# A streaming encoder layer: residual loads, decay rows, head 0 and one head unit change places

## The chip, the core and the metric

The kernel runs on one core of a Trainium2 chip. A core has a matrix engine (TensorE, PE in the profile), a vector engine (DVE), an activation engine (ACT), a general engine (POOL) and a sync engine (SP). Each takes its instructions in the order of its own queue. DMA is issued from the queues of SP, ACT and POOL and carried by 16 DMA engines. The metric is device microseconds of one execution; the time of a kernel is the median of its runs.

## What is computed

One layer of a hybrid encoder with one set of weights, for two request groups: a prompt of 1024 positions and a running stream ("sample") of 32 positions with a cache of 256. Both are handled as 1056 columns of feature-major data.

```
h   = x * (1 + sc1) + sh1
mq, mk, mv, mo, mi, mf, fq, fk, fv, ff, gu, gv = split(h @ w_in)
hm  = mlstm(mq, mk, mv, ...)                    # 4 heads of 64, chunks in sequence
hf  = softmax(fq @ fk.T / 8 + F[t] - F[s]) @ fv # 8 heads of 64, F = cumsum of log forget values
hg  = gu * spatial_gate(layer_norm(gv))
mix = concat(hm, hf, hg) @ w_o
x   = layer_norm(ALPHA * x + (1 + g1) * mix)
y   = (silu(h2 @ w_gate) * (h2 @ w_up)) @ w_down   # h2 = x * (1 + sc2) + sh2
x   = layer_norm(ALPHA * x + (1 + g2) * y)
```

For the sample, the keys, values and log forget values of the cache stand ahead of the new ones, so F there is a running sum over 256 + 32 positions for each of 8 heads. The forgetting attention is called fox in the kernel.

## The kernel before

Nearly every product is made in float32 accuracy from two rounded parts: an operand is split into a high part (a cast, on ACT) and a low part (a subtraction, on DVE), and `gemm` (L110 to L118) makes three matmuls of each 128-row slice. Weights come through `weights` (L92): a load on SP into one of three raw buffers, the cast (L104), the subtraction (L105).

The 1056 columns are two groups: group 0 is positions 0 to 511, group 1 is positions 512 to 1023 and the 32 sample columns. The work goes in phases.

**First phase** (the loop over `ORDER` in `run`). Tokens of `ORDER` are steps: `q3` computes queries and keys of fox head 3 for group 0 (`head_unit`), `f3` is that head's attention over group 0, `g` is the next part of the gates (log forget values, stabilisers), `k0`, `v`, `o`, `G1` and so on are units of the input projection, `s` prepares the mLSTM states, `m0` to `m3` are mLSTM chunks, `a` is a part of the modulation vectors. Results wait in DRAM: `dqh` and `dql` hold queries and keys of the heads, `dv` the values, `dM` the stabiliser rows of the mLSTM, `dmix[c]` the mixers' output of group c, in 8 slices of 128 rows (k = 0, 1 are mLSTM, 2 to 5 fox, 6 and 7 the spatial gate). `head_unit` also makes group 1's part for heads 0 and 1 (`QD = 2`).

**Output projection of group 0** (in `run`, after `s2.close()`). `wo_mix(0, ...)` (L991) loads slices of `dmix[0]` and splits them, six of them first (2, 3, 4, 6, 7, 5), then slices 0 and 1, which come last from the mixers. `wo_res` loads the residual `z` from `xT`, two loads of 1 MB. Between them stand the group 1 units of the fox heads `QD` to `PRE - 1`, that is heads 2 and 3: `fm_unit` (L235) makes a head's queries and keys over 544 columns in 48 matmuls of 272 columns, and `evac_qk` (L358) splits them, stores them in `dqh` and `dql`, and stores the keys as an output. With `act=False` the sum of the two parts and the output store are on POOL, with `act=True` (heads from `PRE` on) on ACT. `wo_range` (L1038) makes the projection in 8 blocks of 128 rows over 256 columns, three PSUM banks deep; `sublayer_end` (L1052) adds the residual, takes a pivot off and sums for the layer norm. The second 256 columns are interleaved with the norm of the first (`ln1`, L1070: scale, shift, modulation, and a new split into operands at L1086 and L1087). The norm of the second half follows, and then the group 1 units of heads `PRE` to 7, which have nothing to do with it.

**Mixers of group 1** (`mixers`) beside the MLP of group 0. After `s1.close()` the memory of the first phase is reused for the attention of group 1. `fox_sample` is the sample's attention: it makes the running sums of the cache's log forget values with a triangular matmul (L853), writes the rows F and -F to DRAM (`dsf`), and reads them back as extra rows of keys and queries (`kn`, `q`, `kc`). Then `fox(h, ...)` runs for heads 0 to 7, for five of them with an mLSTM chunk woven in. The tiles q2, qp, k2 and v have one buffer each there (`foxbufs = (2, 1, 1, 1, 2)`), k1 has two; the sample's q, kn and vc use the tags q2, qp and v. Units of the MLP (`up`, `down`) stand behind the mixers in the program and are PE's filler.

Engines' queues are put in order when the program is built: instructions are taken by priority (program order, with 200 places of advance for steps f and m) as they come ready in a simulated timeline. On the chip that order is fixed, and an instruction that waits holds up what stands behind it on its engine. Tiles with the same tag in a pool share that tag's buffers, and a new tile waits until an older one is let go.

Of the kernel before, what the change touches and what calls it, by code (L numbers as in the profile page):

```python
# [7 lines left out]
F32 = mybir.dt.float32  # L8
F32R = mybir.dt.float32r
AF = mybir.ActivationFunctionType  # L10
ALU = mybir.AluOpType
# [4 lines left out]
P = 128  # L16
D = 1024
KT = 8
S = 1024
T = 1056  # L20
NS = 32
PAST = 256

GO = (0, 512)
GN = (512, 544)
# [6 lines left out]
UPF = 0  # L32
LWE = 1
NB = (3, 2, 2)
PRE = 4
T1 = (1, 1, 0, 2)
XB, AB = (3, 6)
HPA = 200
MLB = (1, 2, 3, 4, 5)
RESE = "pp"  # L40
TAFF = ("aaaaaaaa", "aaaaaaav")
ORDER = "q0 f0 g q1 a f1 a g q2 f2 k0 k1p s a q3 f3 a v q4 f4 a q5 f5 o a m0 G0 q6 f6 a m1 G1p G2p q7 m2 f7 a m3 G3"
FP = (0, 0)
RAW = 3
WB = 3
# [9 lines left out]
def weave(*parts):  # L55

    parts = list(parts)
    while parts:
        for p in list(parts):
            if next(p, parts) is parts:  # L60
                parts.remove(p)
# [6 lines left out]
class Kernel:  # L68
# [10 lines left out]
    def t(self, pool, shape, dt=F32, tag=None, bufs=None):  # L79
        self.n += 1  # L80
        kw = {} if bufs is None else {"bufs": bufs}
        return pool.tile(shape, dt, tag=tag, name=f"{self.phase}_{tag}_{self.n}", **kw)
# [755 lines left out]
        self.store(self.dmix[c][64 * (h % 2):64 * (h % 2) + 64, 2 + h // 2, o:o + nq], r[:, :nq])  # L838


    def fox_sample(self):
        self.phase = "foxs"
        nc, d = self.nc, self.d
        t = lambda shape, tag, bufs=1, dt=F32: self.t(self.mx, shape, dt, tag, bufs)
        N = PAST + NS
        lf = t([P, 2, 8], "lfc")
        self.load(lf, d["cache_lf"])
        lp = t([P, 2, 96], "q2", self.foxbufs[1])
        nc.gpsimd.memset(lp, 0.0)
        nc.vector.tensor_copy(lp[:, :, 64:72], lf)  # L850
        ps = self.t(self.pt, [P, 512], F32, "t")
        for j in range(2):
            nc.tensor.matmul(ps[:96, j * P:(j + 1) * P], lp[:, j, :], self.tri, start=True, stop=True)  # L853
        fr = t([72, 2, N], "p", 4)
        F = fr[64:72, 0, :]
        nc.vector.tensor_copy(F[:, 0:P], ps[64:72, 0:P])
        nc.vector.tensor_scalar(F[:, P:PAST], ps[64:72, P:PAST], F[:, P - 1:P], None, ALU.add)
        nc.vector.tensor_scalar(F[:, PAST:], self.sf[64:72, :], F[:, PAST - 1:PAST], None, ALU.add)
        nc.vector.tensor_scalar(fr[64:72, 1, :], F, -1.0, None, ALU.mult)
        self.store(self.dsf, fr[64:72])  # L860
        q = t([66, 8, NS], "q2", self.foxbufs[1])
        kn = t([66, 8, NS], "qp", self.foxbufs[1])
        for x in (q, kn):
            nc.vector.memset(x[64:66], 1.0)
        nc.vector.tensor_copy(kn[0:64], self.qks[64:128])
        nc.vector.tensor_copy(q[0:64], self.qks[0:64])
        self.load(kn[64:65], self.dsf[:, 1, PAST:].unsqueeze(0))
        self.load(q[65:66], self.dsf[:, 0, PAST:].unsqueeze(0))
        vc = t([P, 2, 512], "v", self.foxbufs[3])
        self.load(vc, d["cache_v"])  # L870
        for g in range(2):
            hs = slice(4 * g, 4 * g + 4)
            kc = t([66, 4, PAST], "k1", self.foxbufs[0])
            nc.vector.memset(kc[64:66], 1.0)
            self.load(kc[0:64], d["cache_k"][:, hs, :])
            self.load(kc[64:65], self.dsf[hs, 1, 0:PAST].unsqueeze(0))
            s = self.t(self.pss, [P, 512], F32, "s")
            for x in range(4):
                r = slice(32 * x, 32 * x + 32)
                nc.tensor.matmul(s[r, :PAST], q[:, 4 * g + x, :], kc[:, x, :], start=True, stop=True)  # L880
                nc.tensor.matmul(s[r, PAST:N], q[:, 4 * g + x, :], kn[:, 4 * g + x, :], start=True, stop=True)
            nc.vector.tensor_tensor(s[:, PAST:N], s[:, PAST:N], self.smask, ALU.add)
            m, z = t([P, 2], "fmx", 3), t([P, 2], "fsm", 3)
            m, z = m[:, 0:1], z[:, 0:1]
            nc.vector.tensor_reduce(m, s[:, :N], AX.X, ALU.max, negate=True)
            pr = t([P, N], "p", 4)
            nc.scalar.activation(pr, s[:, :N], AF.Exp, bias=m, accum_out=z)
            nc.vector.reciprocal(z, z)
            nc.vector.tensor_scalar(pr, pr, z, None, ALU.mult)
            ps = self.t(self.pt, [P, 512], F32, "t")  # L890
            for b in range(3):
                w = P if b < 2 else NS
                nc.tensor.transpose(ps[:w, b * P:(b + 1) * P], pr[:, b * P:b * P + w], self.ident)
            pT = t([P, 3, P], "pth", self.foxbufs[4])
            nc.scalar.copy(pT[:, 0:2, :].rearrange("p b q -> p (b q)"), ps[:, 0:256])
            nc.scalar.copy(pT[0:NS, 2, :], ps[0:NS, 256:384])
            o = self.t(self.po, [P, 512], F32, "o")
            for b in range(3):
                w = P if b < 2 else NS
                for x in range(4):  # L900
                    h = slice(256 * g + 64 * x, 256 * g + 64 * x + 64)
                    nc.tensor.matmul(o[32 * x:32 * x + 32, 0:64], pT[:w, b, 32 * x:32 * x + 32],
                                     vc[:, b, h] if b < 2 else self.vs[:, h], start=b == 0, stop=b == 2)
            ob = t([P, 64], "fo")
            nc.scalar.copy(ob, o[:, 0:64])
            nc.tensor.transpose(o[0:64, P:2 * P], ob, self.ident)
            res = t([64, 2, 2, NS], "fo")
            nc.scalar.copy(res.rearrange("p i a q -> p (i a q)"), o[0:64, P:2 * P])
            for a in range(2):
                self.store(self.dmix[1][64 * a:64 * a + 64, 2 + 2 * g:4 + 2 * g, 512:544], res[:, :, a], nc.scalar)  # L910
# [97 lines left out]

    def wo_res(self, c, pool):
        z = self.z[c] = self.t(pool, [P, KT, GN[c]], F32, f"z{c}", 1)  # L1010
        for k in range(0, KT, 4):
            self.load(z[:, k:k + 4], self.d["xT"][k:k + 4, :, GO[c]:GO[c] + GN[c]].rearrange("k p n -> p k n"))

    def wo(self, c, st, cuts, eng, res=None):
        self.phase = f"wo{c}"
# [301 lines left out]
    def mixers(self):  # L1317
        def slow(part):
            for _ in part:
                yield  # L1320
                yield

        self.fox_sample()
        for h in range(8):
            parts = [self.fox(h, ((4, 5), (6, 7)))]
            if h in MLB:
                parts.append(slow(self.mlstm(self.nextm)))
                self.nextm += 1
            weave(*parts)

    def run(self):
        nc, tc, d = self.nc, self.tc, self.d
        dr = self.pool("dr", space=DRAM)
        t = lambda shape, tag: self.t(dr, shape, F32, tag)
# [72 lines left out]
        def emit(x):  # L1407
            eng = nc.gpsimd if x[-1] == "p" else nc.vector
            x = x.rstrip("p")
            i = int(x[1:] or 0)  # L1410
            if x[0] == "g":
                next(gates, None)
                return ()
            if x[0] == "f":
                return self.fox(i, ((0, 1, 2, 3),))
            if x[0] == "m":
                return self.mlstm(i)
            if x[0] == "q":
                self.head_unit(i)
            elif x[0] == "k":  # L1420
                self.fm_unit(w3[i], self.evac_mqk(2 + i, 0.125), eng=eng)
            elif x[0] == "G":
                self.tm_unit(w2[3 + i % 2], 256, (self.evac_gv, self.evac_gmlp)[i % 2],
                             range(4 * (i // 2), 4 + i // 2 * 5), eng=eng)
            elif x[0] == "s":
                self.mlstm_states()
            elif x[0] == "a":
                more(1)
            else:
                self.tm_unit(w2["-vo".index(x)], 256, self.evac_raw((None, self.dmv, self.dmo)["-vo".index(x)]), eng=eng)  # L1430
            return ()

        for x in ORDER.split():
            if x[0] in "fm" and HPA:
# [10 lines left out]
        self.hh, self.hl, self.z = {}, {}, {}  # L1445
        self.operand(0, self.ph)
        self.wo_mix(0, self.KORDER[0][:6])
        self.wo_res(0, self.pz)
        for h in range(QD, PRE):
            self.fm_unit(w3[2 + h], self.evac_qk(h), (1,))  # L1450
        self.wo_mix(0, self.KORDER[0][6:])
        self.pn = self.pool("pn")
        self.ln_consts()
        st = self.ln_begin(nc.vector)
# [6 lines left out]
        weave(self.ln1(0, st, *MM[0][1]))  # L1461
        for h in range(PRE, 8):
            self.fm_unit(w3[2 + h], self.evac_qk(h, True), (1,))
# [83 lines left out]
        n = nj * 256  # L1547
        t = self.t(self.pz, [P, 4, n], F32R, "z0", 1)
        w = self.last_weights(((t[:, 0], t[:, 1]), (t[:, 2], t[:, 3])), (2, 3))
        act2 = dict(act)  # L1550
        for half, (a, b) in enumerate(LN[1][::-1]):
# [6 lines left out]
            else:  # L1558
                h, l = (self.t(pb, [P, KT * 272], F32R, f"{x}{a}", 1) for x in ("ah", "al"))
# [117 lines left out]
```

## Time and profile before

| | us |
|---|---|
| median of three runs | 1371.85 |
| lowest, highest | 1370.64, 1373.48 |
| the profiled execution | 1378.78 |
| its span | 1376.9 |
| PE busy in it | 1337.6 |
| mean granted clock of PE | 0.991 |

The span is the time from the first to the last instruction in the profiled execution. A line of a timeline gives the start and the length in microseconds, the engine, the line of the kernel, the operation with output and input tiles, the shape, and in brackets how long the engine was idle before and who released it. SPq and POOLq are instructions by which an engine issues DMAs. A stretch gives each engine's busy time with the number of instructions, then the granted clock of PE as a share of full clock, the share of the DMA engines that was busy, and what they moved. Tiles carry the name of the phase in which they were made: `tm_ah` and `tm_al` are the two parts of the projection's operand (their memory was made earlier), `wo_z` is the residual.

### The profile page before, as it was taken

The numbers are of one execution on the slowest core, as the hardware profiler recorded it, in microseconds if no ns is written. First come the engines' busy times: TensorE is split into PE (matmuls) and PEld (weight loads), VectorE is DVE, ScalarE is ACT, GpSimd is POOL, SyncE is SP. The second block draws the span as 40 slices with busy tenths as digits, with TensorE's granted clock in tenths as the row PEclk, the third lists the DMA queues.
The fourth block names the chain that finished last, engine by engine and source line by source line (L and its number), as shares of the span: only waits on it lengthen the run. The fifth ranks groups of instructions, "written<-read, shape, count | busy, mean of one in ns | idle before, by whom it ended". The sixth has DMA issues, their size and how long they took to land.

```text
span 1376.9 us, 25164 instructions
## 1 busy us (share of the span) xinstructions
PE 1337.6 (97%) x9434; PEld 1219.9 (89%) x9434; DVE 997.6 (72%) x2129; ACT 658.2 (48%) x1309; POOL 225.2 (16%) x258
## 2 busy tenths in 40 slices
PE   7999999999999989999999999999999999999996
PEld 4898889998899767888888889899999999999995
DVE  5545553679669648777776766778998988889777
ACT  3314454445436544545545455436564454545354
POOL 0202000053133200000000000274610000000341
PEclk9999999999999989999999999999999999999998
DMA  9765565446444774543433423664596658454321
GB/s 359 257 236 151 159 206 155 164 141 201 149 162 142 199 180 151 148 137 117 144 111 101 128 91 97 199 171 125 175 245 180 195 161 222 133 176 129 99 78 66
DMA packets 119210, 221.72 MB, mean 161 GB/s; under 512 B 18508, under 2 KB 62296, under 8 KB 119088
## 3 DMA queue, kind: packets, MB, share of 16 engines
q1 hardware_dynamic: 111760, 207.55, 47.8%
q0 software_dynamic: 5968, 11.80, 5.0%
q8 instruction: 75, 1.23, 0.4%
q10 hardware_dynamic: 1360, 0.76, 0.2%
q14 instruction: 47, 0.39, 0.1%
HBM read 188.13 MB, written 51.85 MB: 174 GB/s over the span
## 4 chain that ended last, share of the span: by engine, by line
PE 84%; DVE 7%; DMA 5%; ACT 2%; issue 1%; SPq 1%; ACTq 0%; DVEq 0%
PE up_g L116 6%; PE up_g L118 6%; PE up_g L117 6%; PE dn_g L116 4%; PE dn_g L118 4%; PE dn_g L117 4%; PE tm_g L281 3%; PE tm_g L282 3%; PE tm_g L283 3%; PE sup_u L118 3%; PE sup_u L116 3%; PE sup_u L117 3%; PE fox_t L815 2%; PE sup_g L117 2%; PE sup_g L118 2%; PE sup_g L116 2%
## 5 line engine op out<-in xcount | busy, mean ns | idle before, releaser
L116 PE MATMUL up_g<-tm_ah,up_whi 128*128 128x512 f32 (+1 forms) x384 | 141.5, 368 | 1.0 <-ACT start_qks L376 1.0
L118 PE MATMUL up_g<-tm_ah,up_wlo 128*128 128x512 f32 (+1 forms) x384 | 142.1, 370 | 0.0
L117 PE MATMUL up_g<-tm_al,up_whi 128*128 128x512 f32 (+1 forms) x384 | 141.6, 369 | 0.0
L1206 ACT CAST sup_whi<-sup_raw 128x1024 fp32r<-128x1024 f32 x54 | 56.0, 1048 | 91.4 <-PE dn_u L117 47.9
L104 ACT CAST up_whi<-up_raw 128x1024 fp32r<-128x1024 f32 x50 | 52.4, 1049 | 77.6 <-PE dn_g L117 30.9
L116 PEld LDWEIGHTS up_g<-tm_ah,up_whi 128*128 128x128 f32 x384 | 73.1, 190 | 12.4 <-ACT start_qks L376 1.2
L118 PEld LDWEIGHTS up_g<-tm_ah,up_wlo 128*128 128x128 f32 x384 | 73.3, 191 | 10.9
L117 PEld LDWEIGHTS up_g<-tm_al,up_whi 128*128 128x128 f32 x384 | 73.1, 190 | 11.1
L105 DVE TENSOR_TENSOR up_wlo<-up_raw,up_whi 128x1024 fp32r<-128x1024 f32 x50 | 66.8, 1336 | 19.5 <-ACT up_whi L104 19.0
L1061 DVE SCALAR_TENSOR_TENSOR wo_z<-dn_g,start_mod,wo_z 128x512 f32<-128x512 f32 (+4 forms) x120 | 60.1, 520 | 25.3 <-PE dn_g L118 24.9
L788 ACT ACTIVATE fox_p<-fox_s,fox_fmx 128x384 f32<-128x384 f32 (+2 forms) x96 | 55.2, 579 | 46.1 <-DVE fox_fmx L786 37.2
L1207 DVE TENSOR_TENSOR sup_wlo<-sup_raw,sup_whi 128x1024 fp32r<-128x1024 f32 x54 | 68.0, 1262 | 10.4 <-ACT sup_whi L1206 10.3
L116 PE MATMUL dn_g<-up_acth,dn_whi 128*128 128x512 f32 (+2 forms) x200 | 73.8, 370 | 0.0
L118 PE MATMUL dn_g<-up_acth,dn_wlo 128*128 128x512 f32 (+2 forms) x200 | 73.2, 366 | 0.0
L117 PE MATMUL dn_g<-up_actl,dn_whi 128*128 128x512 f32 (+2 forms) x200 | 73.2, 367 | 0.0
L104 ACT CAST dn_whi<-dn_raw 128x1024 fp32r<-128x1024 f32 (+1 forms) x44 | 42.7, 970 | 63.2 <-PE up_g L117 19.8
L783 DVE TENSOR_REDUCE fox_fmx<-fox_s 128x1 f32<-128x384 f32 (+2 forms) x96 | 52.6, 553 | 20.7 <-PE fox_s L780 19.3
L820 ACT CAST fox_pth<-fox_t 128x512 fp32r<-128x512 f32 (+1 forms) x80 | 41.3, 544 | 46.9 <-PE fox_t L815 46.6
L821 DVE TENSOR_TENSOR fox_ptl<-fox_t,fox_pth 128x512 fp32r<-128x512 f32 (+1 forms) x80 | 49.4, 631 | 13.0 <-ACT fox_pth L820 12.4
L105 DVE TENSOR_TENSOR dn_wlo<-dn_raw,dn_whi 128x1024 fp32r<-128x1024 f32 (+1 forms) x44 | 49.5, 1124 | 10.9 <-ACT dn_whi L104 10.5
L281 PE MATMUL tm_g<-tm_whi,start_h1h 128*128 128x256 f32 (+1 forms) x192 | 55.6, 290 | 1.7 <-ACT tm_vhl L711 1.7
L281 PE MATMUL tm_g<-tm_whi,start_ah 128*128 128x256 f32 (+1 forms) x192 | 54.3, 286 | 0.7 <-ACT tm_brs L336 0.7
(659 smaller groups left out, 4816.6 us busy)
## 6 DMA issues: line engine op xcount, KB each, us to landing
up_raw<-w_gu SPq DMA_DIRECT2D x50, 512.0 KB
dn_raw<-w_dn SPq DMA_DIRECT2D x28, 512.0 KB
ada_late<-w_ada SPq DMA_DIRECT2D x24, 512.0 KB
sup_raw<-w_gu SPq DMA_DIRECT2D x20, 512.0 KB
start_dp<-w_gu SPq DMA_DIRECT2D x19, 512.0 KB
start_dp<-w_gu POOLq DMA_DIRECT2D x19, 512.0 KB, 7.5
wo_raw<-w_o SPq DMA_DIRECT2D x18, 512.0 KB
sup_raw<-start_dp SPq DMA_DIRECT2D x18, 512.0 KB
```

The source lines that it names most:

```text
L104: nc.scalar.copy(hi[:, :w], raw[:, :w])
L105: (eng or nc.vector).tensor_tensor(lo[:, :w], raw[:, :w], f(hi[:, :w]), ALU.subtract)
L116: nc.tensor.matmul(ps, hi, xh(k), start=start and k == 0, stop=False)
L117: nc.tensor.matmul(ps, hi, xl(k), start=False, stop=False)
L118: nc.tensor.matmul(ps, lo, xh(k), start=False, stop=stop and k == n - 1)
L281: nc.tensor.matmul(ps[:, :ncol], xh, hi, start=k == 0, stop=False)
L783: nc.vector.tensor_reduce(mxs[:, x:x + 1], s[:, :w], AX.X, ALU.max, negate=True)
L788: nc.scalar.activation(pr[:, lo:hi], banks[x][:, :hi - lo], AF.Exp, bias=mxs[:, 0:1], accum_out=sums[:, x:x + 1])
L821: nc.vector.tensor_tensor(pl[:, :e], ps[:, :e], f(ph[:, :e]), ALU.subtract)
L1061: self.lastz = self.nc.vector.scalar_tensor_tensor(z[:, m, x:y], ps[:, x - a:y - a], g[i], z[:, m, x:y], ALU.mult, ALU.add)
L1206: nc.scalar.copy(h, x)
L1207: tt(l, x, f(h), ALU.subtract)
```

## The change

Four edits:

1. `wo_res(0, ...)` is called after the late head units and after `wo_mix` of the slices 0 and 1, and loads `z` in four loads of 512 KB.
2. `PRE` goes from 4 to 5: the group 1 unit of head 4 is made with those of heads 2 and 3, ahead of the slices 0 and 1, with `act=False`; heads 5 to 7 stay behind the projection.
3. The first part of `fox_sample` becomes `sample_decay`, a step `S` in the first phase after the last part of the gates. Its tiles use the tags `mtot`, `mw` and `mb` of that phase, one buffer each, which the gates and the mLSTM chunks also use. F and -F are stored by two DMAs.
4. In `mixers`, head 0 comes first and the sample attention after it, ahead of head 1.

```diff
-PRE = 4
+PRE = 5
-ORDER = "q0 f0 g q1 a f1 a g q2 f2 k0 k1p s a q3 ...
+ORDER = "q0 f0 g q1 a f1 a g S q2 f2 k0 k1p s a q3 ...
...
+    def sample_decay(self):
+        self.phase = "foxd"
+        nc, N = self.nc, PAST + NS
+        t = lambda shape, tag, bufs: self.t(self.mx, shape, F32, tag, bufs)
+        lp = t([P, 2, 104], "mtot", 1)
+        lf = lp[:, :, 96:104]
+        self.load(lf, self.d["cache_lf"])
+        nc.gpsimd.memset(lp[:, :, 0:96], 0.0)
+        nc.vector.tensor_copy(lp[:, :, 64:72], lf)
+        ps = self.t(self.pt, [P, 512], F32, "t")
+        for j in range(2):
+            nc.tensor.matmul(ps[:96, j * P:(j + 1) * P], lp[:, j, 0:96], self.tri, start=True, stop=True)
+        F, M = (t([72, N], x, 1)[64:72] for x in ("mw", "mb"))
+        nc.vector.tensor_copy(F[:, 0:P], ps[64:72, 0:P])
+        nc.vector.tensor_scalar(F[:, P:PAST], ps[64:72, P:PAST], F[:, P - 1:P], None, ALU.add)
+        nc.vector.tensor_scalar(F[:, PAST:], self.sf[64:72, :], F[:, PAST - 1:PAST], None, ALU.add)
+        nc.vector.tensor_scalar(M, F, -1.0, None, ALU.mult)
+        self.store(self.dsf[:, 0], F)
+        self.store(self.dsf[:, 1], M)
...
     def fox_sample(self):
...
-        lf = t([P, 2, 8], "lfc")
-        self.load(lf, d["cache_lf"])
-        lp = t([P, 2, 96], "q2", self.foxbufs[1])
...
-        fr = t([72, 2, N], "p", 4)
...
-        self.store(self.dsf, fr[64:72])
...
     def wo_res(self, c, pool):
-        for k in range(0, KT, 4):
-            self.load(z[:, k:k + 4], ...)
+        for k in range(0, KT, 2):
+            self.load(z[:, k:k + 2], ...)
...
-        self.fox_sample()
         for h in range(8):
+            if h == 1:
+                self.fox_sample()
...
         self.wo_mix(0, self.KORDER[0][:6])
-        self.wo_res(0, self.pz)
         for h in range(QD, PRE):
             self.fm_unit(w3[2 + h], self.evac_qk(h), (1,))
         self.wo_mix(0, self.KORDER[0][6:])
+        self.wo_res(0, self.pz)
```

More of the change, by code (lines that the diff above doesn't have):

```diff
@@ L41 @@
 TAFF = ("aaaaaaaa", "aaaaaaav")
-ORDER = "q0 f0 g q1 a f1 a g q2 f2 k0 k1p s a q3 f3 a v q4 f4 a q5 f5 o a m0 G0 q6 f6 a m1 G1p G2p q7 m2 f7 a m3 G3"
+ORDER = "q0 f0 g q1 a f1 a g S q2 f2 k0 k1p s a q3 f3 a v q4 f4 a q5 f5 o a m0 G0 q6 f6 a m1 G1p G2p q7 m2 f7 a m3 G3"
 FP = (0, 0)
@@ L845, in fox_sample @@
         N = PAST + NS
-        lf = t([P, 2, 8], "lfc")
-        self.load(lf, d["cache_lf"])
-        lp = t([P, 2, 96], "q2", self.foxbufs[1])
[L849 to L853, printed above, removed]
-        fr = t([72, 2, N], "p", 4)
[L855 to L859, printed above, removed]
-        self.store(self.dsf, fr[64:72])
         q = t([66, 8, NS], "q2", self.foxbufs[1])
@@ L1010, in wo_res @@
         z = self.z[c] = self.t(pool, [P, KT, GN[c]], F32, f"z{c}", 1)
-        for k in range(0, KT, 4):
-            self.load(z[:, k:k + 4], self.d["xT"][k:k + 4, :, GO[c]:GO[c] + GN[c]].rearrange("k p n -> p k n"))
+        for k in range(0, KT, 2):
+            self.load(z[:, k:k + 2], self.d["xT"][k:k + 2, :, GO[c]:GO[c] + GN[c]].rearrange("k p n -> p k n"))
     def wo(self, c, st, cuts, eng, res=None):
@@ L1421, in emit @@
                 self.fm_unit(w3[i], self.evac_mqk(2 + i, 0.125), eng=eng)
+            elif x[0] == "S":
+                self.sample_decay()
             elif x[0] == "G":
```

## The prediction

> **What bounds the kernel now.** I read the head of the page first, then TensorE's (PE's) idle places, then stretches cut at those places.
>
> ```profile
> span 1376.9 us, 25164 instructions
> PE 1337.6 (97%) x9434; PEld 1219.9 (89%) x9434; DVE 997.6 (72%) x2129; ACT 658.2 (48%) x1309; POOL 225.2 (16%) x258
> ```
>
> PE is the bound almost everywhere: 39 us of the span are not PE. The change adds and removes no matmul, so it can only win or lose PE idle time and PE clock. The timeline of PE shows six idle places in the stretch that the change touches (idle time and releaser in brackets):
>
> ```profile
> 371.87 0.39 PE L116 MATMUL wo_g<-tm_ah,wo_whi 128*128 128x256 f32 x1 [1.56 <-ACT wo_whi L104]
> 372.81 0.58 PE L116 MATMUL wo_g<-tm_ah,wo_whi 128*128 128x256 f32 x1 [0.44 <-ACT wo_whi L104]
> ...
> 382.88 0.58 PE L116 MATMUL wo_g<-tm_ah,wo_whi 128*128 128x256 f32 x1 [2.31 <-ACT tm_ah L998]
> ...
> 452.67 0.39 PE L116 MATMUL up_g<-tm_ah,up_whi 128*128 128x256 f32 x1 [0.97 <-ACT start_qks L376]
> ...
> 480.25 0.59 PE L880 MATMUL foxs_s<-foxs_k,foxs_q 66*32 66x256 f32 x5 [1.43 <-DMA foxs_k<-start_dsf]
> ...
> 496.11 0.87 PE L779 MATMUL fox_s<-fox_k,fox_qp 128*128 128x384 f32 x2 [3.86 <-DMA fox_qp<-start_dql]
> ```
>
> Idle: 4.31 us at the start of group 0's output projection, 0.97 at the first up unit, 1.43 before the sample scores, 3.86 before head 0's scores. The stretches around them (PE, weight load, DVE, ACT, POOL busy; then granted clock, DMA share, GB/s):
>
> ```profile
> 370.30:372.60 2.30, 0.51 (x3) 0.30 (x2) 1.25 (x2) 2.21 (x3) 0.80 (x2) 1.00 0.85 192
> 372.60:376.00 3.40, 3.19 (x14) 3.10 (x15) 3.40 (x4) 1.63 (x3) 0.81 (x2) 0.50 0.96 311
> 376.00:380.50 4.50, 4.50 (x40) 4.37 (x39) 0.23 (x1) 0.00 (x0) 0.00 (x0) 1.00 1.05 394
> 380.50:382.85 2.35, 0.06 (x1) 0.00 (x0) 0.00 (x0) 0.64 (x2) 0.00 (x0) 1.00 1.03 407
> 382.85:386.25 3.40, 3.37 (x15) 3.36 (x16) 1.29 (x2) 2.53 (x3) 0.00 (x0) 0.50 0.53 214
> ...
> 478.80:480.25 1.45, 0.02 (x5) 0.03 (x1) 0.00 (x0) 0.77 (x1) 0.00 (x0) 1.00 0.09 33
> 481.85:485.25 3.40, 3.40 (x10) 2.62 (x9) 2.36 (x6) 0.89 (x2) 0.00 (x0) 0.50 0.62 170
> ...
> 496.10:502.30 6.20, 6.04 (x15) 4.71 (x16) 1.51 (x3) 1.04 (x1) 0.00 (x0) 0.50 0.35 83
> ```
>
> Each idle place drags a stretch at half clock behind it: 14 matmuls in 3.40 us against 40 in 4.50 us at full clock. Half clock costs half the stretch: 1.7 us twice at the projection, 1.7 after the sample wait, 3.1 after head 0's. In all the stretch holds 4.31 + 3.4 + 0.97 + 1.43 + 1.7 + 3.86 + 3.1 = 18.8 us that are not work.
>
> [...]
>
> **Late residual loads and the third late head unit.** The SP queue and the chain of waits at the projection:
>
> ```profile
> 370.43 0.94 SPq L85 DMA_DIRECT2D wo_z<-xT  x2
> 371.46 0.46 SPq L89 DMA_DIRECT2D start_dqh<-fm_qkh  x1
> 372.01 0.39 SPq L89 DMA_DIRECT2D start_dql<-fm_qkl  x1
> 372.45 1.31 SPq L85 DMA_DIRECT2D tm_al<-start_dmix  x2
> ```
> ```profile
> 332.48 5.22 DMA tm_al<-start_dmix
> ...
> 372.45 9.73 DMA tm_al<-start_dmix
> ```
>
> Two residual loads (2 MB) stand ahead of the last two slices of the mixer output (k = 0, 1); the DMA engines are full at 394 to 407 GB/s, and the slices take 9.73 us where the earlier ones took 5.22. Now the slices go first: landed at about 372.45 + 5.2 = 377.7, split by 379.
>
> Head 4's unit moves in front. Four such units (192 matmuls) fill the stretch after the projection:
>
> ```profile
> 426.30:451.70 25.40, 25.34 (x196) 24.80 (x196) 22.53 (x53) 19.10 (x44) 8.68 (x9) 1.00 0.50 153
> 452.70:458.50 5.80, 5.80 (x49) 5.80 (x50) 3.72 (x7) 5.54 (x14) 5.20 (x8) 1.00 0.63 194
> ```
>
> One is 25.4/4 = 6.3 us of PE. It covers 370.3 to 376.6, while ACT casts the first weights (they end the 1.56 and 0.44 waits) and the slices land; then the first six slices of three output blocks, 54 matmuls at 4.50/40 = 0.11 us, take PE to 382.7. All three waits and both half-clock stretches should go: **+7.7 us**. Its evacuation falls where ACT, DVE and POOL stand nearly still (0.00 in three cells above). On POOL it adds two sums and two stores, ahead of the residual subtractions, which need the pivot and so the first block anyway. Late next are the four 512 KB residual loads, now behind the slices on SP: from about 373.8, 2 MB at 400 GB/s are 5.2 us, the first quarter in by 377, the last by 381. The first block needs its residual at about 383, so nothing; without that margin it costs up to 2 us.
>
> [...] No run here shows 512 KB residual loads, and the last piece is needed six blocks later.
>
> **What the unit uncovers.** Behind the projection three units are left, 19.1 us, ahead of the layer norm's tail:
>
> ```profile
> L366 DVE SCALAR_TENSOR_TENSOR fm_qkl<-fm_g,start_qsc,fm_qkh 128x272 fp32r<-128x272 f32 x8 | 4.0, 496 | 2.6 <-ACT fm_qkh L365 1.6 <-DMA start_dql<-fm_qkl 1.0
> L105 DVE TENSOR_TENSOR fm_wlo<-fm_raw,fm_whi 128x1024 fp32r<-128x1024 f32 x2 | 2.6, 1320 | 0.1
> ...
> 458.57 0.76 DVE L1087 TENSOR_TENSOR tm_al<-lna_tmp,tm_ah 128x256 fp32r<-128x256 f32 x2 [0.15 <-ACT tm_ah L1086]
> ```
>
> The last operand of the second query half is written at 459.3, 33.0 us after the projection's last matmul (426.3). PE will be through three units and the first half of up unit 0 (5.80, second stretch) at 24.9 us, and needs the last slice some 2.6 us later: 27.5. That is 5.5 us early if the norm keeps its pace. It gets rid of one unit: on DVE 1.32 + 2 x 0.50 = 2.3 us, on ACT about as much, as its cast and evacuations go too. So 2.7 to 3.2 us are open; another up unit's first half (2.9 us for its gate) could stand there. Bounds: 0, or 5.5 and a half-clock stretch, 7.2. I take **-2.7**, the norm relieved but nothing put in. The 0.97 us wait (a bank held by an evacuation on a crowded ACT) goes with the relief: **+1.0**.
>
> **Decay rows early.** The chain at the sample attention:
>
> ```profile
> 465.37 0.61 PE foxs_t L853 x4
> ...
> 471.25 3.70 DMA start_dsf<-foxs_p
> ...
> 476.47 3.65 DMA foxs_k<-start_dsf
> ...
> 488.10 8.90 DMA fox_q<-start_dfs
> ```
>
> The store hop (3.70) leaves this place, the load hop (3.65) stays but can start as soon as its tiles are free: the 1.43 us and their half clock go, **+3.1**. The four matmuls (0.61), five small DVE operations, POOL's clearing, one load and now two stores move to the first phase. PE is full there too, so the matmuls cost nothing on balance. What is queued there is this:
>
> ```profile
> 171.64 7.80 DMA mlstm_mb<-start_dM
> ...
> 179.47 0.69 DVE L615 TENSOR_TENSOR mlstm_mw<-mlstm_mb,start_maskbig 128x512 f32<-128x512 f32 x1 [6.22 <-DMA mlstm_mb<-start_dM]
> ...
> 183.14 0.39 PE L823 MATMUL fox_o<-fox_ptl,head_v 128*64 128x384 f32 x1 [1.09 <-DVE fox_ptl L821]
> ```
>
> The new rows borrow the tiles mb, mw and mtot, one buffer each, between the gates and mLSTM chunk 0. So chunk 0's load of mb must wait for one more store (3.70), DVE stands on it with fox head work behind, and PE, which lost 1.09 us there, may lose up to 3.7 more. The gain bound is those 1.09 us. I take **-1.0**: PE had other units to do through the 6.22 us that DVE stood still.
>
> **Head 0 ahead of the sample attention.** Both draw on the same single buffers (qp, q2, v), so head 0's loads had to wait for the sample scores (8.90 us to landing, 3.86 idle, 3.1 of clock: 7.0). Now they need only the memory that the last head unit leaves. But the sequence has the same number of exchanges: sample to head 1 looks as sample to head 0 did, and PE's order is fixed at build, so it can stand there again. Bounds: +7.0 (the heads' own exchanges show no wait) to -7.0 (a wait at head 0 and at head 1). I take half, **+3.5**, as the new exchange copies the one that stalls, with mLSTM work beside it.
>
> **Sum:** 7.7 + 1.0 - 2.7 + 3.1 - 1.0 + 3.5 = 11.6 us. The profiled execution took 1378.78 (span 1376.9), 6.9 above the median; its forecast is a span of 1365.3, and 1371.85 - 11.6 = **1360** for the median.
>
> **Rivals.**
> - *All waits go*: the tail filled by the next unit, nothing at head 1, none in the first phase: 7.7 + 1.0 + 3.1 + 7.0 = 18.8, **1353**. For it: PE had filler at every later head. Against: 18.8 needs a perfect order.
> - *The wait moves*: the norm's tail stays open (-7.2) and the head exchange keeps its 7.0 at head 1: 7.7 + 1.0 - 7.2 + 3.1 - 1.0 = 3.6, **1368**. For it: 5.5 us of missing cover.
> - *The planner does not follow*: the program's order is only a priority; unit 4 or the slices end up where they were. No 7.7, no -2.7 either: 1.0 + 3.1 + 3.5 - 1.0 = 6.6, **1365**. Against: SP kept the program's order at 370 to 373.
> - *Slower*: PE's fixed order stands at every exchange. Behind the last head unit come head 0, the sample and head 1, each with loads that can start only when its predecessor lets go; where PE's queue has the scores ahead of the landing, each costs what head 0 did, 7.0: 21.0, and the open tail adds 2.7. Against a gain of 18.8 that is 4.9 lost, **1377**. It decides from some 6.3 us per exchange. Against it: later heads show no such wait.
>
> **How the numbers follow.** Forecast 0.52 (own range 1355 to 1366), all go 0.13, wait moves 0.17, planner 0.05, slower 0.13. What counts as no change is 0.2%, 2.7 us: 1369.1 to 1374.6. Faster: 0.52 + 0.13 + 0.05 and over half of the fourth's 0.17, 0.79; slower: most of the last, 0.12; same 0.09. The range 1352 to 1374 leaves out about half of the first and most of the last rival.
>
> **What would show it.** Right: no PE idle over 0.5 us and clock 1.00 from the last first-phase matmul through the projection; the slices' load before the residual's, in about 5 us; no store of decay rows near the sample scores. For the tail: PE idle in front of up unit 0's second half, released by the norm's casts or subtractions. For the exchange: PE idle before head 1's scores on its qp load. Wrong: an idle on residual tiles in the projection's evacuations, or PE idle over 2 us between 165 and 190 us behind mLSTM's mb.

## The result and the profile after

| | before | after |
|---|---|---|
| median of the runs, us | 1372.66 | 1365.72 |
| lowest, highest | 1370.64, 1378.36 | 1362.85, 1367.14 |
| runs | 6 | 6 |
| after / before, 95% interval | | 0.994 [0.9916, 0.9964] |

The medians lie 6.9 us apart; the ratio, which is used below, makes 8.2 us (0.006 x 1373), between 4.9 and 11.5 by its interval: faster, and less than the 11.6 of the prediction. A second set of runs of the same two kernels gave 0.9935 [0.9913, 0.9956].

The head of the page of the kernel after:

```profile
span 1364.7 us, 25185 instructions
PE 1330.3 (97%) x9434; PEld 1215.8 (89%) x9434; DVE 995.4 (73%) x2129; ACT 656.7 (48%) x1306; POOL 226.6 (17%) x263
```

No matmul was added or removed, and PE is as full as before. The timeline of PE in the kernel after, at every idle place over 0.35 us between 340 and 500 us:

```profile
377.99 0.39 PE L116 MATMUL wo_g<-tm_ah,wo_whi 128*128 128x256 f32 x1 [1.18 <-ACT tm_ah L1003]
...
385.11 0.38 PE L116 MATMUL wo_g<-tm_ah,wo_whi 128*128 128x256 f32 x1 [0.57 <-ACT wo_whi L104]
...
386.37 0.39 PE L118 MATMUL wo_g<-tm_ah,wo_wlo 128*128 128x256 f32 x1 [0.76 <-DVE wo_wlo L105]
...
395.71 0.38 PE L118 MATMUL wo_g<-tm_ah,wo_wlo 128*128 128x256 f32 x1 [0.38 <-DVE wo_wlo L105]
...
451.39 0.39 PE L117 MATMUL up_g<-tm_al,up_whi 128*128 128x256 f32 x1 [0.50 <-DVE tm_al L1092]
...
461.21 0.66 PE L779 MATMUL fox_s<-fox_k,fox_qp 128*128 128x384 f32 x1 [4.23 <-DMA fox_k<-start_dqh]
```

Against before: the two waits for the first weights (1.56 and 0.44) are gone, the 2.31 on the last slices is 1.18, and weights of later blocks are waited for instead (0.57, 0.76, 0.38); the 0.97 on a bank is gone and 0.50 on the norm's tail has come; the 1.43 at the sample scores is gone; the 3.86 at head 0 is 4.23, on another load. The stretches at the last slices, at the weights, and at head 0 (busy time of PE, weight load, DVE, ACT, POOL; granted clock, DMA share, GB/s):

```profile
376.80:378.00 1.20, 0.02 (x2) 0.01 (x1) 0.03 (x1) 0.68 (x2) 0.55 (x1) 1.00 1.02 370
378.00:384.50 6.50, 6.50 (x53) 6.28 (x53) 1.56 (x3) 0.82 (x2) 1.52 (x3) 1.00 1.04 409
384.50:386.40 1.90, 0.57 (x4) 0.33 (x3) 1.23 (x1) 1.54 (x3) 0.00 (x0) 1.00 0.75 276
...
459.40:461.20 1.80, 0.00 (x0) 0.02 (x1) 0.00 (x0) 0.00 (x0) 0.00 (x0) 0.50 1.01 225
461.20:463.00 1.80, 1.79 (x8) 1.80 (x9) 0.00 (x0) 0.00 (x0) 0.00 (x0) 0.50 0.93 175
463.00:466.10 3.10, 3.10 (x16) 3.10 (x16) 0.54 (x3) 0.78 (x1) 0.00 (x0) 0.50 1.12 227
```

The projection runs at full clock now (1.00 in its three stretches); only head 0 still has half clock beside it (0.50 from 459.3 to 466.1). What is late at the projection is seen in SP's timeline and in the chain of waits of the kernel after:

```profile
370.80 0.45 SPq L85 DMA_DIRECT2D tm_al<-start_dmix  x1
371.34 3.41 SPq L85 DMA_DIRECT2D wo_z<-xT  x4
374.85 1.42 SPq L85 DMA_DIRECT2D wo_raw<-w_o  x2
```
```profile
369.48 4.66 DMA tm_al<-start_dmix
...
375.76 9.63 DMA wo_raw<-w_o
...
456.86 4.21 DMA fox_k<-start_dqh
```

The slices go first: one takes 4.66 us instead of 9.73, the other, issued at 370.80, is there when ACT splits it at 377.32, after some 6.5. The next weights now stand behind four residual loads in SP's queue and take 9.63.

**Where the time went.** One profiled execution of a kernel differs from another by several us, so both kernels were profiled twice (the second ones are two of the experiments). Read from the first and last matmuls of each stage, in us:

| stage | before | before, again | after | after, again |
|---|---|---|---|---|
| span | 1376.9 | 1369.4 | 1364.7 | 1368.9 |
| start to the first fox scores | 118.2 | 116.2 | 116.5 | 118.0 |
| from there to the last head unit of group 0 | 211.9 | 210.5 | 211.6 | 211.4 |
| from there to the end of group 1's projection | 608.5 | 604.1 | 598.5 | 601.5 |
| the rest | 438.3 | 438.6 | 438.1 | 438.0 |
| PE idle in the fourth row | 13.0 | 11.1 | 9.9 | 10.8 |
| half clock in the fourth row | 17.1 | 10.2 | 6.8 | 10.2 |

The start varies by 2 us in either kernel, and nothing of the change is there. The whole effect is in the fourth row: 6.3 us between the means (606.3 and 600.0). The profile on which the prediction was made has the longest fourth row of the four. Neither pair alone prices the change: the spans differ by 12.2 us in the first and by 0.5 in the second, whose profile of the kernel after is the longest of its six runs (1370.83) and whose profile of before is a short one (1372.53 against a median of 1374.75).

### The profile page after: what moved, and what is told of

The parts are those of the page before. It is cut to its first block, busy times and chain, and to the rows that moved or that the text cites. A ratio compares the mean times of both kernels' runs of the same rounds, so it can differ in the third digit from the quotient of the medians.

```text
span 1364.7 us, 25185 instructions
## 1 busy us (share of the span) xinstructions
PE 1330.3 (97%) x9434; PEld 1215.8 (89%) x9434; DVE 995.4 (73%) x2129; ACT 656.7 (48%) x1306; POOL 226.6 (17%) x263
## 4 chain that ended last, share of the span: by engine, by line
PE 84%; DVE 7%; DMA 5%; ACT 2%; issue 1%; SPq 1%; POOL 1%; DVEq 0%; ACTq 0%
PE up_g L117 5%; PE up_g L118 5%; PE up_g L116 5%; PE dn_g L116 4%; PE dn_g L118 4%; PE dn_g L117 4%; PE tm_g L281 3%; PE tm_g L282 3%; PE tm_g L283 3%; PE sup_u L118 3%; PE sup_u L116 3%; PE sup_u L117 3%; PE fox_t L815 2%; PE sup_g L117 2%; PE sup_g L118 2%; PE sup_g L116 2%
## 5 line engine op out<-in xcount | busy, mean ns | idle before, releaser
L117 PEld LDWEIGHTS up_g<-tm_al,up_whi 128*128 128x128 f32 x384 | 73.1, 190 | 11.1 <-DVE tm_al L1092 0.7
L105 DVE TENSOR_TENSOR up_wlo<-up_raw,up_whi 128x1024 fp32r<-128x1024 f32 x50 | 65.7, 1314 | 11.6 <-ACT up_whi L104 11.0
L105 DVE TENSOR_TENSOR dn_wlo<-dn_raw,dn_whi 128x1024 fp32r<-128x1024 f32 (+1 forms) x44 | 49.5, 1125 | 13.7 <-ACT dn_whi L104 13.2
L282 PE MATMUL tm_g<-tm_wlo,start_h1h 128*128 128x256 f32 (+1 forms) x192 | 55.1, 287 | 0.0
```

Source lines behind the costliest of these rows:

```text
L105: (eng or nc.vector).tensor_tensor(lo[:, :w], raw[:, :w], f(hi[:, :w]), ALU.subtract)
L117: nc.tensor.matmul(ps, hi, xl(k), start=False, stop=False)
L282: nc.tensor.matmul(ps[:, :ncol], xh, lo, start=False, stop=False)
```

## The experiments

Differences between kernels of different sets of runs are taken here from their ratios to before, times 1373 us. By that the change brings 8.2.

**Residual early.** Edit 1 undone (two loads of 1 MB again, and ahead of the slices), the rest of the change kept.

```diff
-        for k in range(0, KT, 2):
+        for k in range(0, KT, 4):
...
         self.wo_mix(0, self.KORDER[0][:6])
+        self.wo_res(0, self.pz)
         for h in range(QD, PRE):
...
-        self.wo_res(0, self.pz)
```

> The changed kernel with its first edit undone: the residual again in two 1 MB loads, ahead of the slices 0 and 1. Theory (head 4's unit is the cover, the place of the residual only decides what waits): the slices take about 9.7 us to land again and cost 1 to 2 us of PE idle, but the weights of the fourth block, which now stood 9.6 us behind the residual, come in time and the 1.7 us idle there goes; together -1 to +1 us against the changed kernel. Rival (the late residual brought the projection's gain): the waits and half-clock stretches come back, +4 us or more.

Measured: 1365.84 us (1364.14 to 1366.92), 0.9927 [0.9906, 0.9948]. PE's timeline has one wait in the place of four, and ACT's shows what led to it:

```profile
380.72 0.39 PE L116 MATMUL wo_g<-tm_ah,wo_whi 128*128 128x256 f32 x1 [2.25 <-DVE fm_qkl L366]
```
```profile
379.64 0.49 ACT L365 ACTIVATE fm_qkh<-fm_g,start_qsc 128x272 fp32r<-128x272 f32 x1 [7.04 <-DMA start_dqh<-fm_qkh]
380.80 1.18 ACT L1003 CAST tm_ah<-tm_al 128x512 fp32r<-128x512 f32 x2 [0.66 <-DMA tm_al<-start_dmix]
```

The one wait is 2.25 us against 1.18 + 0.57 + 0.76 + 0.38 = 2.9. It is not on the last slices: 36 matmuls stand ahead of it, the first six slices of two blocks, and the last slices are split only after it, from 380.80 on. PE waits for DVE's subtraction of the second half of head 4's unit, which ends at 380.67. The units and the blocks share three PSUM banks, and the third block needs the bank that this half holds. ACT stood idle 7.04 us ahead of that half's cast, until the store of an earlier half out of one of the two `qkh` buffers had landed. So the theory had the size right and the cause wrong. The prediction had this evacuation fall where ACT, DVE and POOL stand nearly still; with the residual ahead of it, it is what PE waits for. No run shows the late residual loads, by themselves, to be worth anything: what they save here, the weights behind them give back.

**PRE = 4.** Edit 2 undone (`-PRE = 5`, `+PRE = 4`).

> The changed kernel with head 4's unit behind the projection again. Theory (the unit is the cover of the projection's start): PE stands 2 to 4 us between 368 and 382 us, most likely with a half-clock stretch, and wins back the 0.5 us at the norm's tail; with head 0's scores 16 matmuls later in PE's order, their wait shrinks by about 2 us; +1 to +5 us against the changed kernel. Rival (a unit moved is only a unit moved): within 1 us.

Measured: 1378.28 us (1376.62 to 1380.91), 1.002 [1.0008, 1.0033]: 11 us slower than the change, more than expected. PE's timeline and one stretch:

```profile
386.33 0.58 PE L116 MATMUL wo_g<-tm_ah,wo_whi 128*128 128x256 f32 x1 [3.38 <-ACT wo_whi L104]
...
455.64 0.39 PE L116 MATMUL up_g<-tm_ah,up_whi 128*128 128x256 f32 x1 [2.29 <-ACT start_qks L376]
...
470.66 0.51 PE L779 MATMUL fox_s<-fox_k,fox_qp 128*128 128x384 f32 x1 [2.33 <-DMA fox_k<-start_dqh]
```
```profile
385.60:392.40 6.80, 5.60 (x24) 5.31 (x25) 6.09 (x7) 3.59 (x6) 5.77 (x5) 0.50 0.48 140
```

The waits at the first weights are back (1.56 and 0.45). The slices are not waited for; the fourth block's weights, behind 72 matmuls, are: 3.38 and 0.47, with 6.8 us at half clock, where the change has 0.57 and 0.76 at full clock. That makes 5.9 us of waits and 2.8 of lost clock at the start of the projection, against 2.9 in the change: head 4's unit is what covers this start. The other half of the 11 us is elsewhere. The bank wait of before, 0.97, is 2.29 here, and the scores of head 1 stand 2.05 us on their qp load (526.00), the wait that the prediction feared there; head 0 itself costs less than in the change.

**Sample first.** Edit 4 undone: `self.fox_sample()` stands ahead of `for h in range(8)` again.

> The changed kernel with the sample's attention ahead of head 0 again, decay rows early. Theory (the loads of whatever comes first wait for the memory of the last head unit, and PE's order has its scores too early; a second wait then comes at head 0 as in the kernel before): about 3 to 8 us more than the changed kernel, PE idle before the sample's scores and again before head 0's. Rival (only the memory's release counts, whoever comes first): within 1.5 us, one wait of about 4 us at the sample's scores.

Measured: 1378.14 us (1375.29 to 1381.37), 1.0029 [1.0013, 1.0045], 12 us slower than the change, more than expected. The places in PE's timeline, and the stretch at the first of them:

```profile
458.46 0.58 PE L116 MATMUL up_g<-tm_ah,up_whi 128*128 128x256 f32 x1 [3.85 <-DVE up_sil L1142]
...
473.44 0.42 PE L779 MATMUL fox_s<-fox_k,fox_qp 128*128 128x384 f32 x1 [1.66 <-ACT up_sil L1140]
```
```profile
457.10:467.30 10.20, 8.84 (x60) 7.43 (x61) 4.89 (x12) 2.61 (x7) 1.83 (x3) 0.50 0.65 158
```

The loss is not where head 0 waited before, and neither theory had the place. PE waits 3.85 us for the evacuation of an up unit on DVE (`up_sil`), and then works 8.84 us at half clock: the build has made another order.

**Decay late.** Edit 3 undone: `S` is out of `ORDER`, and the block of `sample_decay` is back at the top of `fox_sample`.

> The changed kernel with the decay rows made inside the sample's attention again, which stays behind head 0. Theory (behind head 0 the store and load hops lie beside some 40 us of head 0 and up units): within 1.5 us of the changed kernel, no PE idle at the sample's scores. Rival (the store hop is on the path wherever the sample stands): +3 us, with PE idle over 1 us before the sample's scores.

Measured: 1374.11 us (1371.5 to 1377.64), 0.9996 [0.9981, 1.0012], 8 us slower than the change. No wait at the sample scores appeared. None appeared in the kernel with the sample first either: edit 3 and edit 4 each take that wait away, so it can't be credited to the early rows alone. The place is group 1's output projection, 400 us later. First the stretch of that projection in the kernel after, then in this kernel, with its slow part:

```profile
877.40:926.60 49.20, 49.20 (x392) 49.04 (x391) 35.32 (x53) 18.09 (x35) 28.40 (x30) 1.00 0.67 172
```
```profile
874.40:932.30 57.90, 54.51 (x392) 52.70 (x392) 43.75 (x64) 20.10 (x40) 33.30 (x33) 0.91 0.72 203
878.60:888.80 10.20, 8.36 (x31) 7.49 (x32) 5.56 (x12) 3.99 (x11) 3.30 (x5) 0.50 0.90 315
```

The same 392 matmuls take 57.9 instead of 49.2 us. The last output of the attention comes 29 us later against the last head unit (540.5 us behind it, in the kernel after 511.6), so that less work stands between the mixers and the projection that needs them. Neither theory had that place. Before has the mixers' end at 532.7 and a projection of 49.1 without a wait, so the late end alone does not bring the stall. The distance from that last output to the projection fits better: 37.8 us in the kernel after and 26.7 in before, without a wait; 14.1 in the two kernels with held scores below, with 2.4 us of waits; 7.4 here. (It is some 20 in the kernel with `PRE = 4` and in the one with the last unit on POOL, without a wait.)

**Head 0's scores held.** The first two up units are emitted ahead of the mixers, and head 0's first scores are put behind the gate half of the second one in PE's order.

```diff
...
+            if h == 0:
+                with self.tc.issue_after(self.gatemm.ins):
+                    next(parts[0])
+                    next(parts[0])
...
-        self.mixers()
...
+        for j in range(2):
+            weave(self.up(0, j, act, pa, WIDE if j else MM[0]))
+            self.ada(20 + j, self.wp, "raw", RAW, self.pg, "g")
+        self.mixers()
...
```

> The changed kernel with the first two up units emitted ahead of the mixers, and head 0's first scores put behind the gate half of the second in PE's order (120 up matmuls ahead of them instead of 80). Theory (PE's order has the scores about 4 us ahead of their loads' landing; nothing else is wrong there): the 4.23 us wait and the 6.8 us half-clock stretch go, 7 us less than the changed kernel, about 1359 us. Rival (a wait of this size belongs to the exchange and moves on): PE stands at the sample's or head 1's scores instead, gain under 2 us.

Measured: 1367.55 us (1366.13 to 1371.6), 0.9947 [0.9925, 0.9969], no gain on the change. In PE's order 120 up matmuls stand ahead of head 0's scores instead of 80, and the 4.23 is gone, but the second product of head 0's scores and its next scores wait:

```profile
465.12 0.44 PE L780 MATMUL fox_s<-fox_k,fox_q 68*128 68x384 f32 x1 [1.75 <-DMA fox_k<-start_dfs]
...
474.56 0.45 PE L779 MATMUL fox_s<-fox_k,fox_qp 128*128 128x384 f32 x1 [2.19 <-ACT fox_p L788]
```

Together 3.94, with 3.4 us at half clock behind the second. The mixers end 22 us later, and group 1's projection loses 2.4 us of idle. The wait moved on, within head 0 and not to the scores that the rival named.

**Last unit on POOL.** Head 7's unit with its sum and key store on POOL: `self.evac_qk(h, True)` becomes `self.evac_qk(h, h < 7)`.

> The changed kernel with the key store of the last head unit (head 7) made on POOL instead of ACT. Theory (head 0's loads wait for memory that the last unit's key store on ACT's queue lets go 9 us after PE has finished that unit): the loads start 3 to 5 us earlier, and with them the landing; PE's order has 96 up matmuls ahead of the scores here, so the wait goes, 5 to 7 us less than the changed kernel. Rival (DMA traffic sets the landing, not the store): loads land at the same time, gain under 2 us, from the order alone.

Measured: 1369.22 us (1366.69 to 1372.31), 0.9962 [0.9948, 0.9976]: 3 us slower than the change. It was meant to let the memory go sooner, and that did not come. In the kernel after, ACT's timeline has the sum and the store of the last keys:

```profile
449.45 0.39 ACT L368 ACTIVATE fm_qkr<-fm_g 64x272 f32<-64x272 f32 x1
449.94 0.48 ACTq L89 DMA_DIRECT2D o_kT<-fm_qkr  x1
```

In this kernel POOL, SP and PE have:

```profile
451.45 4.36 POOL L370 TENSOR_TENSOR fm_qkr<-fm_qkh,fm_qkl 128x272 f32<-128x272 f32 x1 [2.92 <-DVE fm_qkl L366]
...
457.73 0.57 POOL L89 DMA_DIRECT2D o_kT<-fm_qkr  x1
```
```profile
460.17 0.47 SPq L85 DMA_DIRECT2D fox_qp<-start_dqh  x1
```
```profile
466.46 0.66 PE L779 MATMUL fox_s<-fox_k,fox_qp 128*128 128x384 f32 x1 [4.35 <-DMA fox_k<-start_dqh]
```

The store is issued 7.8 us later (457.73 against 449.94) and head 0's first load 6.1 us later (460.17 against 454.06). Of both, 2.9 us are there already at the end of the projection (428.3 against 425.4), so the load is 3.2 us later by the edit. The waits of SP's queue between 440 and 462 us (total, times, longest) say for what, in the kernel after and then in this one:

```profile
SPq L85 <- DMA o_kT<-fm_qkr: 3.4, 1, 3.4
```
```profile
SPq L85 <- DMA o_kT<-fm_qkr: 5.9, 1, 5.9
```

The load waits for the key store to finish: in this kernel the store lands at 460.1 and the load is issued at 460.17. In the nine kernels of this study in which head 0 comes first, its first load comes 2.0 to 4.1 us behind the issue of that store, whatever moved the store. Head 0 costs no more here than in the change (4.35 us and 2.3 of lost clock, 6.6 against 6.7). What this profile has beyond it is a wait of 1.80 at the slices with 3.4 us at half clock, and 1.42 at the norm's tail.

**Residual between blocks.** The late residual in pieces: the first 512 KB as in the change, each further piece behind the weights of later blocks.

```diff
...
+            if a == 0 and m in (1, 3, 5):
+                for i in {1: (2, 3), 3: (4,), 5: (6,)}[m]:
+                    kept[i] = self.weights(self.d["w_o"][i], KT, P, None, pool if i < 3 else None)
+                with self.tc.issue_after(self.lastload.ins):
+                    self.res_piece(m + 1)
...
```

> The changed kernel with the last three residual loads each behind one further block's weights on SP. Theory (2 MB of residual ahead of the fourth block's weights cost the 1.7 us of PE idle at 384 to 396 us): those go, 1 to 2 us less than the changed kernel; the 1.18 us ahead of them shrinks too. Rival (the DMA engines are full either way): within 1 us, the waits move to residual or slices.

Measured: 1363.8 us (1362.53 to 1364.92), 0.9917 [0.989, 0.9945], with no PE idle over 0.4 us between 375 and 423. These are four runs only; a second set stands below.

**Both.** Residual between blocks and head 0's scores held.

> Both of the above edits at head 0 (scores behind 120 up matmuls) and at the projection (residual between the weights). Theory (the two places are independent): the sum of the two gains, 8 to 9 us less than the changed kernel, about 1357 us. Rival (PE's order or a later stage takes part of it back): no better than the held kernel alone.

Measured: 1366.38 us (1364.7 to 1368.09), 0.993 [0.9908, 0.9951]. The gains don't add; group 1's projection has 2.4 us of idle, and there are three half-clock stretches of 3.4 us, at 339, 475 and 882.

**The change again, residual between blocks again, PRE = 6 on top of it, and before again.** In one set, on one chip.

> The changed kernel unaltered, beside the next kernel on one chip. Theory (head 0's scores stand some 7 to 8 us behind the first of its loads, and PE's order is fixed): the wait before them is there again, 3 to 5 us with a half-clock stretch, and the median lies at 1364 to 1367 us. Rival (the wait belonged to one execution): no wait over 1 us there.

> The kernel with the residual loads between the blocks' weights again. Theory (the projection's waits are gone for good): 1 to 3 us less than the unaltered changed kernel, no PE idle over 0.4 us from 368 to 425 us. Rival (the gain was the spread of the runs): within 0.5 us of it.

> The same with head 5's unit moved ahead of the projection too, so that two units are left behind it. Theory (three units were just enough: the norm's tail cost 0.5 us of idle, and a unit is 6.3 us): the tail opens, PE stands 3 to 6 us before the second half of up unit 0 or before head 0's scores, with a half-clock stretch; 4 to 8 us more than with three. Rival (the norm keeps up because it has fewer evacuations beside it): within 1.5 us.

> The kernel before, unaltered. Theory (the 18.8 us of waits and half clock between 368 and 502 us are what its order costs in each execution): the same six waits within 1.5 us each, clock stretches included. Rival (the first profile caught a bad execution): two or more of the waits missing, span about 1370 us.

| | median, us | lowest, highest | to before |
|---|---|---|---|
| the change again | 1365.87 | 1363.92, 1370.83 | 0.9935 [0.9913, 0.9956] |
| residual between blocks | 1365.81 | 1363.06, 1370.23 | 0.9935 [0.9909, 0.996] |
| with PRE = 6 | 1371.25 | 1368.44, 1377.15 | 0.9977 [0.996, 0.9994] |
| before, one run beside 17 others (median 1374.75) | 1372.53 | | |

Residual between blocks is the same as the change: its 1363.8 did not come again, and no version is shown to beat the change. Its profile had these waits, in PE's timeline:

```profile
380.70 0.50 PE L116 MATMUL wo_g<-tm_ah,wo_whi 128*128 128x256 f32 x2 [1.06 <-ACT tm_ah L1003]
...
460.77 0.41 PE L779 MATMUL fox_s<-fox_k,fox_qp 128*128 128x384 f32 x1 [3.56 <-DMA fox_k<-start_dqh]
```

The weights' waits are gone, the slices' is there. With one more unit moved ahead only two are left behind the projection, 48 up matmuls stand ahead of head 0's scores, and the wait there grows, as expected (the projection has 1.85 us on DVE's `wo_z` besides, at 389.68):

```profile
456.27 0.66 PE L779 MATMUL fox_s<-fox_k,fox_qp 128*128 128x384 f32 x1 [5.68 <-DMA fox_k<-start_dqh]
```
```profile
453.20:463.40 10.20, 6.19 (x32) 4.35 (x33) 7.49 (x21) 7.31 (x17) 5.91 (x8) 0.50 1.11 231
```

The wait at head 0 is as firm in the change (4.23 and 3.81) as in before. Before again, and the change again, in PE's timelines:

```profile
368.73 0.39 PE L116 MATMUL wo_g<-tm_ah,wo_whi 128*128 128x256 f32 x1 [1.56 <-ACT wo_whi L104]
...
379.01 0.38 PE L116 MATMUL wo_g<-tm_ah,wo_whi 128*128 128x256 f32 x1 [1.50 <-ACT tm_ah L998]
...
475.12 0.45 PE L880 MATMUL foxs_s<-foxs_k,foxs_q 66*32 66x256 f32 x4 [0.60 <-DMA foxs_q<-start_dsf]
...
489.16 0.66 PE L779 MATMUL fox_s<-fox_k,fox_qp 128*128 128x384 f32 x1 [3.58 <-DMA fox_qp<-start_dql]
```
```profile
464.16 0.41 PE L779 MATMUL fox_s<-fox_k,fox_qp 128*128 128x384 f32 x1 [3.81 <-DMA fox_k<-start_dqh]
```

All waits of the first profile of before are there again, those at the slices and the sample smaller by 0.8 each. No half clock follows the sample's, and 3.4 us of it instead of 6.8 follow head 0's.

## Why the prediction was right in sign and range, and where its sum was off

Each term with what two pairs of profiles show (before and after; the two taken again). Lost clock is counted only where PE works in it: half the length (in before, matmuls of 256 columns started 0.21 us apart at 0.50, from 373.8 to 375.9, and 0.11 apart at 1.00 right behind).

| term | predicted | first pair | second pair |
|---|---|---|---|
| start of the projection | +7.7 | 7.7 - 2.9 = +4.8 | 6.9 - 2.9 = +4.0 |
| bank wait, norm's tail | +1.0 - 2.7 | 0.97 - 0.50 = +0.5 | +0.5 |
| sample's exchange | +3.1 | +3.1 | +0.6 |
| first phase | -1.0 | +0.3 | -0.9 |
| head 0 | +3.5 | 7.0 - 6.7 = +0.3 | 5.8 - 5.5 = +0.3 |

- **Start of the projection, direction right, too large.** Unit 4 covers the first weights, as the run with PRE = 4 shows by taking the cover away. The step that failed is "All three waits and both half-clock stretches should go". The stretches did, and the two waits at the first weights; the one at the slices only shrank, and three at later weights came. The prediction had PE busy to 382.7 with the first six slices of three blocks, 54 matmuls, as in before; in the order of the changed kernel 21 stand ahead of the last slice, seven slices of one block, so PE was there 1.18 us before it was split, at 377.99 (379 in the prediction). And the residual was named as late next, but the fourth block's weights were: their load stands behind four residual loads on the queue. The prediction looked at who needs the 2 MB, and not at what waits behind them. Two loads of 1 MB, put early, gave 1365.84 and four of 512 KB, put late, 1365.72. Size and place changed together there, so no run shows what the size alone is worth.
- **Norm's tail, bounded rightly, sized too high.** The tail costs 0.50 us where -2.7 was taken, and the released bank gives its 0.97. The two made +0.5, not -1.7.
- **Sample's exchange, right in place and kind.** The wait and its half clock are gone in both profiles of the change, though not by the early rows alone (see *Decay late*). What they cost depends on the profile: 3.1 in one, 0.6 in the other.
- **First phase, nothing to see.** The idle of 1.09 us is gone, but before again does not have it either, and the stage is 0.3 shorter in one pair and 0.9 longer in the other. Chunk 0's load of mb does come later, at 192.00 instead of 171.64, behind the stores of the decay rows at 186.16 and 186.69; DVE stands on it 3.65 us (6.22 in before), and PE has no wait over 0.3 us there.
- **Head 0, as large an error.** Half of 7.0 was taken between two bounds; what came is nothing, in both pairs. The prediction said that head 0's loads now "need only the memory that the last head unit leaves". That was the wait: the loads come 2.0 to 4.1 us behind the last key store, which ends that unit's evacuation, and the scores stand only 80 up matmuls behind the unit in PE's order. Its own warning, that the order is fixed and the wait can stand again at an exchange, was right, but it placed that wait at head 1, where the change has none. Holding the scores back moved the wait on, so whether any order of this work avoids it stays open.

In the first pair these terms make 9.0 us, in the second 4.5. That 9.0 lies so near the 11.6 is in part luck: the start and head 0 were taken 6.1 us too high, the norm's tail and the first phase 3.5 too low. The change again also has a wait of 1.06 with a half-clock stretch beside the sample scores (2.8 together), and its wait at the spatial gate, untouched by the change, is 2.28 with a half-clock stretch at 338 where before again has 1.68 and none (2.3 more). The stage table also leaves 1.4 and 2.2 us less time of PE at work in the fourth row, idle and lost clock taken off; the four moved decay matmuls are 0.6 of it, the rest was not traced to an edit.

The second error is in the basis. The 18.8 us that were to be won come from a profiled execution that ran 6.9 us above the median, and the sum was taken off the median. By the same count the other profile of before has 1.56 + 0.44 + 1.50 + 3.4 + 0.97 + 0.60 + 5.8 = 14.3, where 5.8 is 3.58 and 0.53 at head 0's first and next scores and 1.7 of clock. Some 4.5 us of the waits were that execution's own. The forecast of its span, 1365.3, came out at 1364.7, but not by these terms: 1.7 of the 12.2 us between the spans are the start, which varies by as much in either kernel, and 1.4 are not traced.

Of the rivals, "the wait moves" named the right thing, a head exchange that keeps its price, at the wrong head, and had 1368. "The planner does not follow" had 1365, the number that came, by chance: the planner did follow, with unit 4 and the slices in front. "Slower" did not come for the change, but three single edits undone show that it can: they cost 11, 12 and 8 us, where the whole change brings 8.2. So the edits are no sum of parts, and the terms above are a bookkeeping of places, not of edits.

## What to carry to other kernels

A load that is moved back can make late what is issued behind it on its queue (here the weights behind the four residual loads took 9.63 us to land, and PE stood 0.57 and 0.76 us on the fourth block's): list that first, then who needs the moved data. The new phase's wait for memory went here with the last store of the old one (head 0's first load came 2.0 to 4.1 us behind the issue of that store), not with the end of its matmuls. Where the order is made anew at each build, price edits by the whole kernel, and take the waits from two profiles before counting them as gain.

## What was not expected of the hardware

**Half clock came on a grid.** In each profile all changes of the granted clock lie a whole number of 3.413 us apart. In before half clock begins at 372.61, 382.85, 481.84 and 495.49: 3, 29 and 4 steps; in the change again at 338.52, 464.81 and 505.77: 37 and 12. Counted by these steps, half clock followed PE's idle time in the step before: in before, 1.80, 2.29, 1.43 and 3.24 us of it ahead of those four, while full clock followed 0.97 us (451.12 to 454.53). Over all 14 profiles, between 300 and 600 us, all 17 steps at full clock with 1.88 us or more of PE idle were followed by a step at half clock, 6 of 18 with 1.4 to 1.88, 1 of 25 with 0.95 to 1.4, and none of 1125 with less. Between 0.95 and 1.88 us the idle time alone did not decide, and what else did is not shown. So an idle place could be split by the grid or not, and a wait of much the same length cost up to 1.7 us more in one run than in another: before had the sample's 1.43 us within one step and paid; the 2.36 us at head 0 in the first run of residual between blocks lay across two, as 0.70 and 1.66, and the 3.56 us in the second run as 1.72 and 1.84, and neither cost any clock. The prediction took every idle place to drag half clock behind it.

**One POOL sum took 4.36 us.** In the run with the last unit on POOL one of the twelve sums of 128 x 272 elements took 4.36 us, beside back-to-back work of DVE (450.20 to 457.51). The other eleven took 0.76 to 1.65, in the middle 0.77, and the longest of any other run 1.83. It happened once; that DVE's work caused it was not tested.
